# A fused attention-and-convolution block: convolution taps on ScalarE and by adding transfers, and the seven-product pairs regrouped

## The chip, the cores and the metric

The kernel runs on one core of one Trainium2 chip. The metric is the device time of one execution in microseconds (us). TensorE is called PE in the profile, its weight loads PEld, VectorE DVE, ScalarE ACT, GpSimd POOL, and SyncE SP; SP issues most transfers, and POOL issues those that add to what stands in their destination.

## What is computed

One layer over 256 rows (two halves of 128, called h) of width 4096:

```python
xn = rms_norm(h, norm_in_g[i])
proj = xn @ w_in[i]
q, k, v, z_a, a_c, g_c, z_c = jnp.split(proj, ...)
y_a = chunked_attention(q.reshape(shp), k.reshape(shp), v.reshape(shp), rel_table[i])
y_a = rms_norm(y_a, attn_out_g[i]) * jax.nn.silu(z_a)
y_c = conv_module(a_c, g_c, w_dw[i], b_dw[i], conv_ln_g[i], conv_ln_b[i], w_pw[i], b_pw[i])
y_c = rms_norm(y_c, conv_out_g[i]) * jax.nn.silu(z_c)
h = h + jnp.concatenate([y_a, y_c], axis=-1) @ w_out[i]
gate = jax.nn.sigmoid(rms_norm(h, ple_norm_g[i]) @ w_ple_gate[i] + b_ple_gate[i])
h = h + gate * (p[i] @ w_ple[i])
return rms_norm(h, final_g)
```

The module that the change touches is the convolution: `u = a * sigmoid(g)`, then a causal depthwise convolution of 31 taps for each of 2048 channels, a layer norm over the channels, silu, and the product with `w_pw`.

## The kernel before, in words

All large products run on PE as fp32r. A weight tile `wt` of 128 rows and two 512-column blocks comes from memory (SP), ACT casts it to a high part `wh`, DVE subtracts to get the low part `wl`, and PE adds three matmuls of 128x512 (high by high, low by high, high by low) per block. `wpool` holds three `wh` and three `wl`, so the casts run at most a few matmul groups ahead of PE.

`mixed_product` walks over 16 pairs of row blocks in an order written out by hand (`early`, `early_six`, ...). A plain pair takes eight block products, 24 matmuls. A pair with a mark takes seven, 21 matmuls, for which sums of weight blocks (`ua`, `ub`) and combined left operands (`comb`, `comb_x`) are needed. With `*` DVE adds up the weight sums; with `+` an SP transfer fetches the first operand of `ua` and a POOL transfer adds the second to it (`sums_ahead`), and DVE does the rest.

The order of the work is this: the products for the convolution input (`glu_conv(0)` and `(1)`), queries and keys 0, values 0 and 1, attention 0, `glu_conv(2)`, queries and keys 1, attention 1, `glu_conv(3)`, queries and keys 2, queries 3 and values 2, attention 2, `layer_norm_swish`, keys 3 and values 3 (order `norm`), attention 3, and then the product with `w_pw`, whose left operand `uS` is what the layer norm and silu leave. `attention(g)` handles four heads one after the other: scores (two `kT,qT` matmuls per head), DVE adds the bias and finds the maximum, ACT takes the exponential, PE transposes, ACT copies (`pT`), PE multiplies with the values, and ACT scales.

Small work waits in a queue, `later`. After every pair of a product, `fill(n)` takes n entries from its front and writes them into the program; the numbers stand in tables such as `early_fills`, one number per pair. Each `glu_conv` puts 124 entries in it, four blocks of 31 taps (`conv_tap`, each one DVE instruction that multiplies a shifted row by a tap and adds). `layer_norm_swish` puts 71 in it, the last of which are 16 swish entries (a DVE multiplication and an ACT silu each) and 16 split entries (an ACT cast and a DVE subtraction each, which make `uS`). What is still in the queue after attention 3 is written out there, by `fill(len(later))`. A scheduler then sets each engine's order from this program, and each engine works through its own list in that order.

Of the kernel before, what the change touches and what calls it, by code (L numbers as in the profile page):

```python
# [25 lines left out]
def hybrid_block(  # L26
# [23 lines left out]
    nc = tc.nc  # L50
    _, T, D = x.shape
# [5 lines left out]
    TAPS = w_dw.shape[1]  # L57
    PAD = TAPS - 1
# [215 lines left out]
    def sum_rows():  # L274
        return [spool.tile([P, NB], F32, tag="row", name="comb", bufs=3) for _ in range(2)]
# [92 lines left out]
    norm_fills = (7, 8, 8, 8, 6, 4, 2, 3, 2, 3, 2, 2, 0, 6, 5, 5)  # L368
    final = units("1 0* 3 2* 5 4* 6* 7 8* 9 10* 12* 11 13 14 15")
# [2 lines left out]
    def spare_places(tiles):  # L372

        return [[t[:, 0, q, P:] for q in range(2)] for t in tiles]

    places = {}

    def combine_into_places(pair, tiles):

        rows = sum_rows()  # L380
        places[pair] = spare_places(tiles[:4])
        t, i = tiles[pair // 2], pair % 2 * 2
        combine_again(None, None, t, i, rows, at_places=places[pair])()

    def mixed_product(
        w, col, lhs, comb, order, on_helpers, ahead=None, fills=(0,), on_begin=None, apart=NB,
# [252 lines left out]
    def combinations(c, then=lambda ins: None):  # L639
# [8 lines left out]

        return begin, lambda: rest.pop()()

    def first_pairs(add):


# [82 lines left out]
        nc.vector.tensor_reduce(r_x, ssq_x, AX.X, ALU.add)  # L736
        rsqrt(r_x, r_x, D)
        later.extend(combinations(0))
        return n_x + 1, behind

    rows = [(conv_ln_g, KCW), (conv_ln_b, KCW), (b_dw, KCW), (attn_out_g, AW // P),
# [46 lines left out]

    def conv_tap(cv, uT, i, b, k):
        if k == PAD:  # L790
            nc.vector.tensor_scalar(
                cv[:, i, :], uT[:, i, :], dw[:, b, k : k + 1], bdw[:, b : b + 1], ALU.mult, ALU.add
            )
        else:
            nc.vector.scalar_tensor_tensor(  # L795
                cv[:, i, PAD - k :], uT[:, i, : T + k - PAD], dw[:, b, k : k + 1],
                cv[:, i, PAD - k :], ALU.mult, ALU.add,
            )

    def comb_place(where, tag, **kw):  # L800
        return where.tile([P, 2, 2, T], F32R, tag=tag, name="comb_x", **kw), 0

    def more_combinations(pair):

        if pair in (7, 9, 11):
            c = (pair + 1) // 2
            xS[2 * c] = comb_place(act, "act") if c < 6 else comb_place(spool, "hd", bufs=5)
            later.extendleft(reversed(combinations(c)))

    def glu_conv(c):  # L810
        if c == 0:
            sg, gate = scaled_pair(
                w_in0, o_a, o_g - o_a, first, r_x, (1,), begin=first_pairs
            )
        else:
            sg, gate = scaled_pair(
                w_in0, o_a + c * NB, o_g - o_a,
                *((early, r_x, early_fills) if c == 1 else (early_seven, r_x, seven_fills)),
                ahead=more_combinations if c == 2 else None,
            )  # L820
# [303 lines left out]
    r_c = rstd_of(ssq_c, CW, "r_c")  # L1124


    xS = [xS[0][0]]
    for c in range(2, D // NB):
        if c % 2 == 0:
# [306 lines left out]
```

## Time and profile before

| what | value |
|---|---|
| time, median of 3 runs (lowest, highest) | 2023.68 us (2023.65, 2024.45) |
| the profiled execution: time / span | 2023.59 us / 2021.8 us |
| granted TensorE clock, mean | 0.997 |
| PE busy | 2003.7 us, 99% of the span |
| DVE busy | 1920.5 us, 95% |
| ACT busy | 1259.6 us, 62% |
| POOL busy | 75.8 us, 4% |
| transfers | 450.86 MB, 223 GB/s on average |

How to read it: the profiled execution is 0.09 us below the median, and 1.8 us of it lie outside the span. A matmul's record is longer (about 390 ns) than the distance from one matmul to the next, since matmuls overlap. Lines such as L428 are lines of the kernel before; most matmuls come from one helper and share L428.

Windows of the profile in this text go by stages: 97.6 us is the end of `glu_conv(0)`'s product, 889.9 us the end of the product for keys 3 and values 3, and attention 3 lies between 893 and 914 us.

### The profile page before, as it was taken

Reading aid. Unit: us, or ns where it says so; the run is one execution under the profiler, and the core shown is the slowest. Engines: PE = TensorE matmul, PEld = TensorE weight load, DVE = VectorE, ACT = ScalarE, POOL = GpSimd, SP = SyncE. Lnnn points to the kernel's source line nnn. Section 1 sums busy time; section 2 is a strip of 40 time slices with the busy share of each in tenths; the row PEclk is TensorE's granted clock in tenths of the full one; section 3 lists DMA queues with packets and bytes.
Section 4 is the critical chain, followed back from the end, with each engine's and each line's share of the span. In section 5 each row is a group of like instructions: output and inputs, shape, how many; then the busy total and the mean of one; then the engine's idle time right before and its main releaser. Section 6 shows DMA issues by size and latency. Waiting matters only on the chain.

```text
span 2021.8 us, 26364 instructions
## 1 busy us (share of the span) xinstructions
PE 2003.7 (99%) x9043; PEld 1650.4 (82%) x9043; DVE 1920.5 (95%) x2759; ACT 1259.6 (62%) x1634; POOL 75.8 (4%) x83
## 2 busy tenths in 40 slices
PE   9999999999999999999999999999999999999997
PEld 7888888878888888788888888888888888888885
DVE  7999999899999999888999999999999999999997
ACT  7655555665666556776566676776666766566564
POOL 0000000000000000000000000000000000000000
PEclk9999999999999999999999999999999999999998
DMA  8788878678668877556686786876767766767675
GB/s 292 224 233 241 249 221 251 179 220 259 200 198 256 255 201 241 161 178 206 204 238 213 221 244 203 255 232 203 242 209 238 231 197 208 237 214 237 219 238 172
DMA packets 175920, 450.86 MB, mean 223 GB/s; under 512 B 14494, under 2 KB 17710, under 8 KB 175786
## 3 DMA queue, kind: packets, MB, share of 16 engines
q1 hardware_dynamic: 161952, 417.93, 63.6%
q0 software_dynamic: 13184, 30.41, 8.8%
q8 instruction: 71, 1.16, 0.2%
q10 hardware_dynamic: 650, 0.84, 0.1%
q14 instruction: 63, 0.52, 0.1%
HBM read 441.78 MB, written 4.19 MB: 221 GB/s over the span
## 4 chain that ended last, share of the span: by engine, by line
PE 93%; DVE 3%; DMA 2%; issue 2%; ACT 1%; POOLq 0%; POOL 0%; ACTq 0%; DVEq 0%
PE acc L428 70%; PE acc_P L428 18%; PE tmp_ps L170 1%; DVE wl L205 1%; PE acc L245 1%; DMA wt<-in_w_in_dram 1%; DVE cv L795 1%; DMA low<-in_w_in_dram 0%; DVE ul L205 0%; PE tmp_ps L967 0%; PE tmp_ps L951 0%; PE tmp_ps L985 0%; PE tmp_ps L990 0%; DMA wt<-in_w_ple_dram 0%; DMA wt<-in_w_ple_gate_dram 0%
## 5 line engine op out<-in xcount | busy, mean ns | idle before, releaser
L428 PE MATMUL acc<-wh,big_t 128*128 128x512 f32 x4028 | 1240.7, 391 | 0.9 <-DVE z L1146 0.9
L204 ACT CAST wh<-wt 128x1024 fp32r<-128x1024 f32 (+1 forms) x716 | 684.2, 965 | 460.9 <-PE acc L428 336.0
L428 PEld LDWEIGHTS acc<-wh,big_t 128*128 128x128 f32 x4028 | 753.5, 188 | 156.5 <-issue 1.0
L205 DVE TENSOR_TENSOR wl<-wt,wh 128x1024 fp32r<-128x1024 f32 (+1 forms) x716 | 787.9, 1112 | 30.0 <-ACT wh L204 24.8
L428 PE MATMUL acc<-wl,big_t 128*128 128x512 f32 x1958 | 760.3, 392 | 0.2 <-DVE wl L205 0.2
L428 PEld LDWEIGHTS acc<-wl,big_t 128*128 128x128 f32 x1958 | 367.4, 188 | 77.3 <-DVE wl L205 1.5
L204 ACT CAST uh<-ua 128x1024 fp32r<-128x1024 f32 x187 | 196.7, 1052 | 125.3 <-DVE ua L527 71.2
L205 DVE TENSOR_TENSOR ul<-ua,uh 128x1024 fp32r<-128x1024 f32 x187 | 228.0, 1219 | 6.7 <-ACT uh L204 5.1
L795 DVE SCALAR_TENSOR_TENSOR cv<-uT,dw,cv 128x255 f32<-128x255 f32 (+23 forms) x480 | 203.2, 461 | 1.1
L428 PE MATMUL acc_P<-uh,big_t 128*128 128x512 f32 x570 | 175.4, 389 | 0.0
L204 ACT CAST uh<-ub 128x1024 fp32r<-128x1024 f32 x99 | 104.2, 1053 | 51.6 <-DVE ub L540 36.8
L428 PEld LDWEIGHTS acc_P<-uh,big_t 128*128 128x128 f32 x570 | 107.0, 188 | 22.2
L205 DVE TENSOR_TENSOR ul<-ub,uh 128x1024 fp32r<-128x1024 f32 x99 | 120.7, 1219 | 0.5
L428 PE MATMUL acc_P<-ul,big_t 128*128 128x512 f32 x285 | 111.1, 390 | 0.0
L526 DVE TENSOR_TENSOR ua<-wt 128x512 f32<-128x512 f32 x112 | 76.7, 685 | 12.6 <-DMA wt<-in_w_in_dram 6.3
L428 PE MATMUL acc<-uh,big_t 128*128 128x512 f32 x286 | 88.5, 389 | 0.0
L428 PE MATMUL acc_P<-wh,big_t 128*128 128x512 f32 x286 | 88.2, 390 | 0.0
L527 DVE TENSOR_TENSOR ua<-wt 128x512 f32<-128x512 f32 x112 | 76.7, 685 | 4.7 <-DMA wt<-in_w_in_dram 3.5
L428 PE MATMUL acc_P<-uh,comb_t 128*128 128x512 f32 x228 | 70.2, 390 | 0.2 <-ACT uh L204 0.2
L540 DVE TENSOR_TENSOR ub<-ub,wt 128x512 f32<-128x512 f32 x99 | 68.1, 688 | 1.6
L539 DVE TENSOR_TENSOR ub<-ua,wt 128x512 f32<-128x512 f32 x99 | 67.7, 684 | 0.0
L428 PEld LDWEIGHTS acc_P<-ul,big_t 128*128 128x128 f32 x285 | 53.5, 188 | 12.1 <-DVE ul L205 1.0
(254 smaller groups left out, 1634.2 us busy)
## 6 DMA issues: line engine op xcount, KB each, us to landing
wt<-in_w_in_dram SPq DMA_DIRECT2D x416, 512.0 KB, 4.7
wt<-in_w_out_dram SPq DMA_DIRECT2D x128, 512.0 KB, 4.4
wt<-in_w_ple_gate_dram SPq DMA_DIRECT2D x128, 512.0 KB, 4.4
wt<-in_w_pw_dram SPq DMA_DIRECT2D x32, 512.0 KB, 4.5
ua<-in_w_in_dram SPq DMA_DIRECT2D x31, 512.0 KB, 4.3
ua<-in_w_in_dram POOLq DMA_DIRECT2D x31, 512.0 KB, 8.7
wt<-in_w_in_dram SPq DMA_DIRECT2D x31, 256.0 KB, 2.8
low<-in_w_in_dram POOLq DMA_DIRECT2D x12, 512.0 KB, 8.5
```

What stands on the lines that cost most here:

```text
L170: nc.tensor.transpose(pt[:, i * T + h * P : i * T + (h + 1) * P], src[:, h, b] if len(src.shape) == 4 else src[:, h, b * P : (b + 1) * P], ...
L204: nc.scalar.copy(wh[:, :kc, :], wt[:, :kc, :]),
L205: nc.vector.tensor_tensor(wl[:, :kc, :], wt[:, :kc, :], wh[:, :kc, :].bitcast(F32), ALU.subtract),
L245: nc.tensor.matmul(acc, a, b[:, k, :], start=kb == 0 and kind == 0, stop=kb == kblocks - 1 and kind == 2,)
L428: nc.tensor.matmul(banks[name], a, b, start=name not in begun, stop=final and ends[name] == n and kind == 2 and not (left and name in "P2 ...
L526: plus(ua[:, 0], w0[:, 0], w0[:, 1])
L527: plus(ua[:, 1], w0[:, 1], w1[:, 1])
L539: plus(ub[:, 0], ua[:, 0], w1[:, 1])
L540: plus(ub[:, 1], ub[:, 0], w1[:, 0])
L795: nc.vector.scalar_tensor_tensor(cv[:, i, PAD - k :], uT[:, i, : T + k - PAD], dw[:, b, k : k + 1], cv[:, i, PAD - k :], ALU.mult, ALU.add,)
```

## The change

It does four things.

- A block's first tap moves from DVE to ACT. For two of the four blocks of each group, eight taps more become an ACT instruction that writes a scaled, shifted row to a tile `tap` (two buffers, tag `pT`, which attention's `pT` also uses), and a POOL transfer that adds `tap` to `cv`. These rounds stand in `later` after every third DVE tap.
- The operand for pair 8 is combined early, at the end of the first product (`early_places`), so that pair 8 can be a seven from `glu_conv(1)` on; pairs 10 and 12 are combined in `glu_conv(2)` and `glu_conv(3)`.
- The orders change: five sevens instead of four in `glu_conv(1)`, in queries and keys 0 and in values 0 and 1; six instead of seven in `glu_conv(2)`; four as before for queries and keys 1 and 2, the last of them with `*` instead of `+`.
- The fill tables change.

The core of the diff, with what is unchanged or follows from it left out:

```diff
-    early = units("1 3 5 0+ 7 9 2+ 11 13 4+ 15 8 6+ 10 12 14")
-    early_five = units("1 3 5 0+ 7 9 2+ 11 4* 13 6+ 15 8* 10 12 14")
+    early = units("1 3 5 0+ 7 9 2+ 11 13 4+ 15 8 6* 10 12 14")
+    early_five = units("1 3 5 0+ 7 9 2+ 11 8* 13 4+ 15 10 6* 12 14")
...
-    early_fills = (5, 6, 1, 5, 6, 1, 5, 6, 1, 5, 6, 1, 2, 5, 5, 4)
-    six_fills = (6, 6, 1, 5, 1, 5, 1, 5, 1, 5, 1, 5, 1, 6, 7, 7)
-    seven_fills = (6, 6, 1, 5, 1, 5, 1, 5, 1, 5, 1, 2, 5, 2, 5, 7)
+    five_fills = (5, 5, 1, 4, 5, 1, 4, 1, 5, 1, 4, 5, 1, 2, 5, 5)
+    third_fills = (5, 5, 4, 4, 4, 4, 5, 4, 4, 4, 4, 4, 4, 4, 5, 6)
+    early_fills = (5, 6, 1, 5, 5, 1, 5, 5, 1, 5, 5, 1, 2, 5, 4, 4)
+    six_fills = (6, 5, 1, 5, 1, 5, 1, 5, 1, 4, 1, 5, 1, 5, 6, 6)
+    seven_fills = (6, 5, 1, 5, 1, 5, 1, 5, 1, 5, 1, 2, 5, 2, 4, 7)
...
+    def early_places():
...
+            rows = spool.tile([P, 2, NB], F32, tag="stage", name="comb")
+            two = spool.tile([P, 2, 2, P], F32R, name="comb_p", bufs=1)
+            homes = spare_places(xT[:2]) + [[two[:, i, q] for q in range(2)] for i in range(2)]
+            rest.append(combination_in_places(8, xT, (rows[:, 0], rows[:, 1]), homes))
...
         if k == PAD:
-            nc.vector.tensor_scalar(
-                cv[:, i, :], uT[:, i, :], dw[:, b, k : k + 1], bdw[:, b : b + 1], ALU.mult, ALU.add
+            nc.scalar.activation(
+                cv[:, i, :], uT[:, i, :], AF.Identity,
+                scale=dw[:, b, k : k + 1], bias=bdw[:, b : b + 1],
             )
...
+    BY_DMA = 8
...
+    def tap_by_dma(cv, uT, c, i, shift):
+
+        b = 4 * c + i
+        t = spool.tile([P, T], F32, tag="pT", name="tap")
+        nc.scalar.activation(
+            t[:, shift:], uT[:, i, : T - shift], AF.Identity,
+            scale=dw[:, b, PAD - shift : PAD - shift + 1],
+        )
+        nc.gpsimd.dma_start(cv[:, i, shift:], t[:, shift:], accum_op=ALU.add)
...
-    def more_combinations(pair):
-        if pair in (7, 9, 11):
...
+    early_groups = {
+        1: (early_five, r_x, five_fills, None),
+        2: (early_six, r_x, third_fills, more_combinations(9, 10)),
+        3: (early_seven, r_x, seven_fills, more_combinations(11, 12)),
+    }
...
-        for i in range(4):
-            for k in reversed(range(TAPS)):
-                later.append(partial(conv_tap, cv, uT, i, 4 * c + i, k))
+        chain = {i: [partial(conv_tap, cv, uT, i, 4 * c + i, k) for k in reversed(range(TAPS))] for i in range(4)}
+        later.extend(chain[i].pop(0) for i in range(4))
+        rounds = deque((i, shift) for shift in range(1, BY_DMA + 1) for i in (2, 3))
+        for i in (2, 3):
+            del chain[i][:BY_DMA]
+        for n, work in enumerate(chain[0] + chain[1]):
+            later.append(work)
+            if n % 3 == 2 and rounds:
+                later.append(partial(behind_cast, tap_by_dma, cv, uT, c, *rounds.popleft()))
+        later.append(partial(behind_tap, chain[2].pop(0)))
+        later.extend(chain[2])
...
-    heads((o_q, 0), (o_k, 0))
-    heads((o_v, 0), (o_v, 1))
+    heads((o_q, 0), (o_k, 0), order=early_five, fills=five_fills)
+    heads((o_v, 0), (o_v, 1), order=early_five, fills=five_fills)
...
-    moved = comb_place(spool, "hd", bufs=5)
-    nc.scalar.copy(moved[0], xS[10][0])
-    xS[10] = moved
```

What stands in the engines' lists differs at three places of interest. The first is PE's list in attention 3. Before, from the transposes (`ident,s`) of one head to the scores (`kT,qT`) of the next, `acc` being the banks of the product with `w_pw`:

```order
L985 MATMUL tmp_ps<-ident,s 128x128
L428 MATMUL acc_8125<-wh,big_t 128x512 x2
L985 MATMUL tmp_ps<-ident,s 128x128 x2
L428 MATMUL acc_8125<-wl,big_t 128x512
L428 MATMUL acc_8127<-wh,big_t 128x512 x2
L990 MATMUL tmp_ps<-z,pT 128x128
L991 MATMUL tmp_ps<-z,pT 128x128
L992 MATMUL tmp_ps<-z,pT 128x128
L966 MATMUL tmp_ps<-kT,qT 128x128
L967 MATMUL tmp_ps<-kT,qT 128x256
L428 MATMUL acc_8127<-wl,big_t 128x512
```

And PE's list there now, from the layer norm's last small product (`lnsum,mean_w`) and the transposes of the keys (`ident,z`) to the second head's scores:

```order
L960 MATMUL tmp_ps<-lnsum,mean_w 128x128 x2
L1007 MATMUL tmp_ps<-ident,z 128x128 x8
L1022 MATMUL tmp_ps<-kT,qT 128x128
L1023 MATMUL tmp_ps<-kT,qT 128x256
L1041 MATMUL tmp_ps<-ident,s 128x128 x3
L1046 MATMUL tmp_ps<-z,pT 128x128
L1047 MATMUL tmp_ps<-z,pT 128x128
L1048 MATMUL tmp_ps<-z,pT 128x128
L1022 MATMUL tmp_ps<-kT,qT 128x128
```

The matmuls of the product with `w_pw` that stood between the steps of the first three heads are gone from there: before, 59 of them stood ahead of the fourth head's last step, now 14, all in the fourth head.

The second place is ACT's list in attention 3, before, from the copy of the keys through the first head's exponentials (L978) to its last step (L994):

```order
L956 COPY kT<-tmp_ps 128x512 x2
L298 CAST comb_u<-comb 128x2x256
L978 ACT_TABLE_LOAD
L978 ACTIVATE s,den<-s,nm 128x128
L978 ACTIVATE s,den<-s,nm 128x256
L204 CAST wh<-wt 128x1024
L987 COPY pT<-tmp_ps 128x384
L298 CAST comb_u<-comb 128x2x256
L204 CAST wh<-wt 128x1024
L994 ACTIVATE qT<-tmp_ps,den 128x128 x2
```

And now; L966 is the swish entries' silu, which stood ahead of attention 3 before, and L1034 the exponential:

```order
L1012 COPY kT<-tmp_ps 128x512 x2
L966 ACT_TABLE_LOAD
L966 ACTIVATE cv<-cv,prm 128x256
L1034 ACT_TABLE_LOAD
L1034 ACTIVATE s,den<-s,nm 128x128
L1034 ACTIVATE s,den<-s,nm 128x256
L966 ACT_TABLE_LOAD
L966 ACTIVATE cv<-cv,prm 128x256
L1043 COPY pT<-tmp_ps 128x384
L966 ACTIVATE cv<-cv,prm 128x256 x3
L1050 ACTIVATE qT<-tmp_ps,den 128x128 x2
L966 ACTIVATE cv<-cv,prm 128x256 x2
```

The 16 silus now stand between the four heads' exponentials, with eight table loads up to the fourth head's exponential where there was one, and the split casts behind the third head.

The third place is POOL's list from the start, before, with the adding transfers for `ua`:

```order
L134 MEMSET mhalf 128x2
L139 TENSOR_TENSOR r_x<-r_x,mhalf 128x2
L471 DMA ua<-in_w_in_dram 128x2x512 x6
L1017 MEMSET bias 64x4x64
L471 DMA ua<-in_w_in_dram 128x2x512 x11
```

And now, where `tap` are the new adding transfers:

```order
L139 TENSOR_TENSOR r_x<-r_x,mhalf 128x2
L476 DMA ua<-in_w_in_dram 128x2x512 x2
L837 DMA cv<-tap 128x255 x2
L837 DMA cv<-tap 128x254 x2
L476 DMA ua<-in_w_in_dram 128x2x512
L837 DMA cv<-tap 128x253 x2
L837 DMA cv<-tap 128x252 x2
L837 DMA cv<-tap 128x251
L476 DMA ua<-in_w_in_dram 128x2x512
```

Sixteen `tap` transfers per group of channels now share POOL's list with the `ua` transfers.

More of the change, by code (lines that the diff above doesn't have):

```diff
@@ L376, in hybrid_block, with combination_in_places @@
     places = {}
+    def combination_in_places(pair, tiles, rows, homes):
+        places[pair] = homes
+        t, i = tiles[pair // 2], pair % 2 * 2
+        return combine_again(None, None, t, i, rows, at_places=homes)
     def combine_into_places(pair, tiles):
[L380 to L383, printed above, removed]
+        combination_in_places(pair, tiles, sum_rows(), spare_places(tiles[:4]))()
     def mixed_product(
@@ L738, in first_pairs @@
         later.extend(combinations(0))
+        later.extend(early_places())
         return n_x + 1, behind
@@ L790, in conv_tap, with behind_tap, comb_place, more_combinations @@
         if k == PAD:
-            nc.vector.tensor_scalar(
-                cv[:, i, :], uT[:, i, :], dw[:, b, k : k + 1], bdw[:, b : b + 1], ALU.mult, ALU.add
-            )
-        else:
[L795 to L801, printed above, removed]
-    def more_combinations(pair):
-        if pair in (7, 9, 11):
-            c = (pair + 1) // 2
-            xS[2 * c] = comb_place(act, "act") if c < 6 else comb_place(spool, "hd", bufs=5)
-            later.extendleft(reversed(combinations(c)))
+            nc.scalar.activation(
+                cv[:, i, :], uT[:, i, :], AF.Identity,
+                scale=dw[:, b, k : k + 1], bias=bdw[:, b : b + 1],
+            )
+        else:
+            last_tap[:] = [
+                nc.vector.scalar_tensor_tensor(
+                    cv[:, i, PAD - k :], uT[:, i, : T + k - PAD], dw[:, b, k : k + 1],
+                    cv[:, i, PAD - k :], ALU.mult, ALU.add,
+                )
+            ]
+    BY_DMA = 8
+    last_tap = []
+    def behind_tap(work):
+        with tc.issue_after(last_tap[0].ins):
+            work()
+    def tap_by_dma(cv, uT, c, i, shift):
[4 more added lines that the diff above has]
+            scale=dw[:, b, PAD - shift : PAD - shift + 1],
+        )
+        nc.gpsimd.dma_start(cv[:, i, shift:], t[:, shift:], accum_op=ALU.add)
+    def comb_place(where, tag):
+        return where.tile([P, 2, 2, T], F32R, tag=tag, name="comb_x"), 0
+    def more_combinations(at, new):
+        def ahead(pair):
+            if pair == at:
+                xS[new] = comb_place(act, "act")
+                later.extendleft(reversed(combinations(new // 2)))
+        return ahead
+    early_groups = {
[3 more added lines that the diff above has]
+    }
     def glu_conv(c):
@@ L817, in glu_conv @@
                 w_in0, o_a + c * NB, o_g - o_a,
-                *((early, r_x, early_fills) if c == 1 else (early_seven, r_x, seven_fills)),
-                ahead=more_combinations if c == 2 else None,
+                *early_groups[c][:3], ahead=early_groups[c][3],
             )
@@ L838, in glu_conv @@
         cv = act.tile([P, 4, T], F32, tag="act", name="cv")
-        for i in range(4):
-            for k in reversed(range(TAPS)):
-                later.append(partial(conv_tap, cv, uT, i, 4 * c + i, k))
+        chain = {i: [partial(conv_tap, cv, uT, i, 4 * c + i, k) for k in reversed(range(TAPS))] for i in range(4)}
[9 more added lines that the diff above has]
+        later.extend(chain[2])
+        later.append(partial(behind_tap, chain[3].pop(0)))
+        later.extend(chain[3])
         conv.append(cv)
@@ L1124, in hybrid_block @@
     r_c = rstd_of(ssq_c, CW, "r_c")
+    places.pop(8)
     xS = [xS[0][0]]
```

3 lines of the change are left out of this document (added).

## The prediction

> **What bounds the kernel now.** I read the page's busy times first, then the stages' windows, then PE's waits, then the chain of waits around attention 3, the stage that the order of instructions says is rearranged most.
>
> ```profile
> span 2021.8 us, 26364 instructions
> PE 2003.7 (99%) x9043; PEld 1650.4 (82%) x9043; DVE 1920.5 (95%) x2759; ACT 1259.6 (62%) x1634; POOL 75.8 (4%) x83
> ...
> PE 93%; DVE 3%; DMA 2%; issue 2%; ACT 1%; POOLq 0%; POOL 0%; ACTq 0%; DVEq 0%
> ```
>
> PE is busy all but 18.1 us, and 93% of the chain that ended last is PE. DVE at 95% looks like a second bound. What DVE costs PE is read from the nine stages between the end of the first product (97.6 us) and the end of the product for keys 3 (889.9 us), which hold all the convolution taps; the columns are the window, its length, then each engine's busy time:
>
> ```profile
> 183.40:268.90 85.50, 85.50 (x383) 70.80 (x382) 85.50 (x141) 44.28 (x50) 5.17 (x5) 1.00 0.82 240
> ...
> 794.70:889.90 95.20, 94.82 (x443) 77.21 (x442) 84.36 (x141) 71.58 (x120) 1.64 (x1) 1.00 0.56 179
> sum 792.30, PE 790.40 PEld 650.13 DVE 764.49 ACT 461.93 POOL 39.40; mean PE 87.82 PEld 72.24 DVE 84.94 ACT 51.33 POOL 4.38
> ```
>
> In the second row shown first, queries and keys 0, PE and DVE are both busy for 85.5 of 85.5 us; over all nine PE is idle for 792.3 - 790.4 = 1.9 us. Its named waits there are as small:
>
> ```profile
> PE acc_P L428 <- ACT uh L204: 1.6, 3, 0.9
> PE acc_P L428 <- DVE ul L205: 0.2, 1, 0.2
> PE acc L428 <- DVE wl L205: 0.2, 1, 0.2
> ```
>
> So DVE keeps up, just. Relief for DVE can return about 2 us there and no more; only fewer matmuls shorten these stages. Now attention 3, by the chain in order of time (start, length, what):
>
> ```profile
> 893.33 0.49 PE tmp_ps L966 x2
> ...
> 900.10 0.22 PE tmp_ps L966 x2
> ...
> 904.71 0.22 PE tmp_ps L966 x2
> ...
> 909.32 0.22 PE tmp_ps L966 x2
> ...
> 913.14 0.35 PE tmp_ps L990 x2
> 913.49 0.22 PE tmp_ps L991 x2
> 913.72 0.22 PE tmp_ps L992 x2
> 913.94 8.43 PE acc L428 x37
> ```
>
> ```profile
> 893.30:913.90 20.60, 20.57 (x110) 16.52 (x111) 14.11 (x34) 15.14 (x35) 0.00 (x0) 1.00 0.41 134
> ```
>
> Heads start at 893.3, 900.1, 904.7 and 909.3, and PE is through with the fourth at 913.9. The window over all four says that PE is busy for 20.57 of 20.60 us: matmuls of the next product (acc) fill each head's waits. The chain's last row gives the distance of matmuls: 8.43 / 37 = 0.228 us.
>
> **The change, part by part.**
>
> *Sevens.* Marked pairs of the ten products before attention 3 go from 47 to 49 (five instead of four in three products, six instead of seven in one). Each saves three matmuls: 6 x 0.228 = 1.4 us gained. All of it counts, as PE is full there.
>
> *Taps off DVE, sums onto it.*
>
> ```profile
> L795 DVE SCALAR_TENSOR_TENSOR cv<-uT,dw,cv 128x255 f32<-128x255 f32 (+23 forms) x480 | 203.2, 461 | 1.1
> L526 DVE TENSOR_TENSOR ua<-wt 128x512 f32<-128x512 f32 x112 | 76.7, 685 | 12.6 <-DMA wt<-in_w_in_dram 6.3 <-DMA wt<-in_w_ple_gate_dram 4.5 <-DMA wt<-in_w_out_dram 1.6
> L205 DVE TENSOR_TENSOR ul<-ua,uh 128x1024 fp32r<-128x1024 f32 x187 | 228.0, 1219 | 6.7 <-ACT uh L204 5.1 <-PE acc L428 1.2
> L156 ACT ACTIVATE big_t<-tmp_ps,prm 128x256 fp32r<-128x256 f32 x64 | 27.7, 470 | 4.1 <-DVE big_t L157 2.5 <-PE tmp_ps L170 1.6
> hc<-z POOLq DMA_DIRECT2D x12, 256.0 KB, 6.1
> ```
>
> 80 taps at about 0.46 us leave DVE (37 us); 18 more additions for weight sums (12.3 us) and four more low parts (4.9 us) come, so it is relieved by some 20 us in 792. PE gets back about half of its 1.9 us: 1 us gained, between 0 and 1.9.
>
> *Taps on ACT and POOL.* 80 ACT instructions, nearest row 0.47 us, are 38 us, beside 330 us of ACT idle in those stages. The 64 adding transfers are half as large as the 256 KB ones that land after 6.1 us; with two `tap` buffers the tap after next waits in ACT's list for a landing, with weight casts queued behind it. A fill hands out about one round per pair (some 5 us), so the tap after next comes about 10 us later than the first and the landing is in time. Five fewer `ua` transfers pay for part of the traffic. I take 0. From the other side: if one round in each of the four groups is late by a whole landing and PE sees a third of it, that costs 4 x 6.1 / 3, some 8 us.
>
> *The queue runs over.* This decides. The queue receives 4 x 124 tap entries, 71 of the layer norm, and two for each later combination. Before: 573 entries, and the fill tables take 5 x 64 + 58 + 58 + 63 + 71 = 570, so 3 are left at attention 3. Now: 571 entries, and the tables take 3 x 54 + 70 + 60 + 56 + 60 + 58 + 71 = 537. 34 are left: all 16 swishes and 16 splits. They make `uS`, which the product with `w_pw` reads, so its matmuls can no longer fill the heads' waits, and PE's list has none ahead of the fourth head. ACT's list has the silus between the exponentials instead, with a table load at each switch. Durations of these, from ACT's order of time before:
>
> ```profile
> 893.18 0.59 ACT L956 COPY kT<-tmp_ps 128x512 f32<-128x512 f32 x1
> ...
> 894.41 1.28 ACT L978 ACT_TABLE_LOAD   x1
> 895.71 0.40 ACT L978 ACTIVATE s<-s,nm 128x128 f32<-128x128 f32 x1
> ...
> 896.51 0.18 ACT L978 ACTIVATION_READ_ACCUMULATOR s<-s,nm 128x1 f32 x1
> ```
>
> ```profile
> 844.81 1.58 ACT L910 ACTIVATE cv<-cv,prm 128x256 f32<-128x256 f32 x3
> ```
>
> ```profile
> 882.28 1.63 ACT L920 CAST big_t<-cv 128x256 fp32r<-128x256 f32 x5
> ```
>
> ```profile
> 914.13 0.62 ACT L994 ACTIVATE qT<-tmp_ps,den 128x128 f32<-128x128 f32 x2
> ```
>
> ```profile
> L987 ACT COPY pT<-tmp_ps 128x384 f32<-128x384 f32 x16 | 7.7, 478 | 9.7 <-PE tmp_ps L985 9.7
> ```
>
> ACT has the copy of the keys behind it at 893.8. Then, by its new list: load 1.28, one silu 0.6, load 1.28, so the first exponential starts 3.2 us later. From there to the second: exponentials 0.98 (895.71 to 896.69), load 1.28, silu 0.5, copy 0.48, three silus 1.58, the pair of L994 0.62, two silus 1.1, load 1.28: 7.8, less four overlaps of 0.1 (five casts take 1.63): about 7.5 us instead of the 4.6 us from head to head before. The same to the third, 7.2 to the fourth (four splits, 1.3, stand for three silus), then 0.9 of exponentials, three splits 0.9 and the copy, 2.3. Sum 3.2 + 7.5 + 7.5 + 7.2 + 2.3 = 27.7, so 921.5; with the last head's products (0.8, the rows at 913.14) and 0.1 to start them PE is through at 922.4 instead of 913.9: 8.5 us lost. Moreover 59 filling matmuls were done by then and now 14: 45 x 0.228 = 10.3 us to do afterwards. Behind the fourth head's copy ACT has six splits (2.0), two squares (nearest row the copy of 512 columns, 0.59, and a read of 0.18 each), two casts of 512 columns (1.2) and the pair of L994 before the next weight cast (1.2, twice 0.59), 6.5 us, and DVE's low part (1.2) behind it; PE has 0.9 and 22 matmuls, 5.9 us. Between 0 and 1.8 us lost; 1.5, since most of the matmuls there need the cast first.
>
> Table loads at a switch have a page: the Trainium skill (ScalarE: Activation LUTs, What ACT_TABLE_LOAD costs) gives 1.28 us and 1.38 us of drain for a switch of tables. The trace agrees on the load and shows no drain: the exponential starts 0.02 us after it. By the page's 2.66 us, seven more loads would cost another 9.7 us, 2051.1 in all; an estimate that I don't use.
>
> *Sum:* -1.4 - 1.0 + 8.5 + 10.3 + 1.5 = +17.9 on the profiled execution's 2023.59 (0.09 below the median): **2041.5 us**.
>
> **The rivals.**
>
> *A, the forecast:* 2041.5. For it speak the lists, which each engine keeps to. Chance 0.58.
>
> *B, the heads keep their pace of 4.6 us.* Then ACT's silus and loads hide and only the missing filling matmuls cost: 2023.59 + 10.3 - 2.4 = 2031.5. Against it, ACT was idle for 20.6 - 15.1 = 5.5 us there, too little for 16 silus (8 us) and seven more loads (9 us). Chance 0.07.
>
> *C, not slower.* PE would have to get back, in the nine tap stages, what attention 3 loses, by DVE waits that vanish: the chain's 3% of DVE are 60 us on paper. It decides from 17.9 us on, which gives 2023.6. Against it, PE's idle time there is 1.9 us, and the whole span's 18.1. Chance 0.04.
>
> *D, PE's clock falls in attention 3.* For some 20 us PE has only small matmuls, with a gap of some 3.5 us before each head's transposes (ACT's 1.58 + 0.62 + 1.1 + 1.28 + 0.4, less 1.5 of PE's own work). The span's first matmuls of 512 columns, after idleness, are long:
>
> ```profile
> L125 PE MATMUL tmp_ps<-idle 128*128 128x512 bf16 x10 | 4.8, 628 | 1.2 <-DVE ssq_f L1241 1.2
> ```
>
> 628 against some 390 ns. With 0.24 us more for each of the first 15 matmuls afterwards (3.6 us) and 0.5 per head: 2041.5 + 5 = 2046.5. The Trainium skill (TensorE: Matmul & The Clock Gate, Part 1) has a rule to this effect: half the clock after about 3.4 us of idleness, until as long a busy stretch; by it D holds if a gap covers a whole window of its monitor. No run here shows that at the page's figures. Chance 0.22.
>
> *E, the taps' transfers are late*, ACT's casts wait behind them, PE behind those: up to 2041.5 + 8 = 2049.5. POOL's list alternates `tap` with `ua` transfers that wait for SP. Chance 0.09.
>
> **How the numbers follow.** The measurement tells a change of about 0.2%, 4 us, from none. A, B, D and E all lie above that; C's 0.04 is split, 0.02 no change and 0.02 faster, and 0.01 of B goes to no change. Slower 0.95. The low end of the range, 2033, lies between B and A and allows 8 us for steps of ACT that overlap better; the high end, 2052, takes in D and E one at a time. What is left out is B, C and the two together, under 0.2.
>
> **What would show it.** In the profile after: the nine tap stages' lengths within 2 us of before (sevens, E); four heads about 7.5 us apart, PE busy for under a third between the first and the fourth, its transposes waiting for ACT's `s` and its value products for `pT`; 16 table loads instead of 10; a distance of 0.23 us at the first matmuls after the fourth head (against D). I am wrong if the first `w_pw` matmuls stand between the first heads, if the heads are 4.6 us apart, or if the stages before attention 3 shrink by more than 5 us.

## The result: 2.5% slower, and where the time went

The changed kernel takes 2073.69 us (median of four runs, 2071.72 to 2074.24) against 2023.78 for the kernel before beside it: ratio 1.0245, interval 1.0228 to 1.0261. It is 50 us slower; 17.9 were forecast. The profiled execution took 2071.72 us. Its page, the span, the busy times and the chain's engines (the chain reaches back only to 726 us of the span, so its shares don't compare with the 93% of PE before):

```profile
span 2069.9 us, 26521 instructions
...
PE 2019.7 (98%) x9037; PEld 1654.6 (80%) x9037; DVE 1915.3 (93%) x2704; ACT 1296.2 (63%) x1726; POOL 124.7 (6%) x142
...
PE 56%; DVE 4%; ACT 2%; issue 1%; DMA 1%; POOLq 0%; POOL 0%; ACTq 0%; DVEq 0%
```

Six matmuls are gone (9043 to 9037), and PE is idle for 50.2 us instead of 18.1. The same windows as before, from the end of the first product to the end of the ninth stage, show where (queries and keys 0, queries and keys 2, the sum):

```profile
187.20:277.40 90.20, 84.98 (x371) 68.19 (x370) 78.90 (x111) 46.92 (x55) 8.31 (x9) 1.00 0.80 231
...
639.90:734.20 94.30, 89.42 (x385) 72.79 (x384) 84.81 (x135) 51.18 (x64) 11.95 (x13) 0.96 0.84 231
...
sum 817.40, PE 798.67 PEld 650.22 DVE 743.82 ACT 478.04 POOL 88.58; mean PE 88.74 PEld 72.25 DVE 82.65 ACT 53.12 POOL 9.84
```

DVE was relieved by 20.7 us, as computed, yet the nine stages grew from 792.3 to 817.4. PE idles there for 18.7 us instead of 1.9, and in the second row its clock is at 0.96. What is left, from the end of the ninth stage (914.7) to the end of the span, takes 1155.2 us instead of 1131.9. So the loss in this profile is 25.1 us in the tap stages and 23.3 behind them. The waits in the stages, after (total, times, longest):

```profile
DVE wl L205 <- ACT wh L204: 39.7, 28, 7.3
...
ACT tap L833 <- DMA cv<-tap: 30.0, 12, 7.4
...
PE acc L433 <- ACT wh L204: 5.8, 2, 4.8
...
DVE cv L815 <- DMA cv<-tap: 4.5, 4, 3.0
```

The first was 4.8 us before, in the same columns:

```profile
DVE wl L205 <- ACT wh L204: 4.8, 10, 1.3
```

Those on the taps' transfers (`cv<-tap`) are new. The longest of them, in order of time on POOL, ACT and PE:

```profile
713.01 1.23 POOL L476 DMA_DIRECT2D ua<-in_w_in_dram  x1 [9.56 <-DVE z L589]
713.75 1.43 POOL L837 DMA_DIRECT2D cv<-tap  x1
722.42 0.86 POOL L837 DMA_DIRECT2D cv<-tap  x1 [7.23 <-issue]
```

```profile
709.05 0.91 ACT L833 ACTIVATE tap<-uT,dw 128x254 f32<-128x254 f32 x2
...
723.60 0.51 ACT L833 ACTIVATE tap<-uT,dw 128x253 f32<-128x253 f32 x1 [7.44 <-DMA cv<-tap]
...
725.23 1.97 ACT L204 CAST wh<-wt 128x1024 fp32r<-128x1024 f32 x2
```

```profile
721.09 0.39 PE L433 MATMUL acc<-wl,big_t 128*128 128x512 f32 x1
726.31 1.22 PE L433 MATMUL acc<-wh,big_t 128*128 128x512 f32 x2 [4.84 <-ACT wh L204]
```

ACT wrote two taps, at 709.05 and 709.47. POOL's list had a `ua` transfer ahead of theirs, which waited until 713.01. The first tap's transfer, right behind it, landed 9.8 us after its issue, at 723.5; the second's went out at 722.42 only, 0.3 us after the `ua` transfer had landed. ACT's next tap needs the first tile back and waits 7.4 us, the weight copies behind it wait too, and PE stands still. This pattern comes four times in the nine stages, each time where a tap's transfer is issued right behind a `ua` transfer of 512 KB: it lands after 8.2 to 10.4 us (the median of all 64 is 5.0), and POOL's next transfer goes out 0.3 us after the `ua` transfer's landing. Why POOL holds that one back is not shown (the profile says "issue"). The eight tiles of these transfers came back 9.4 to 15.1 us after ACT had written them, the other 56 within 7.6 us. Behind the stall PE runs at half clock, as the windows around it show (PEclk is the third number from the end):

```profile
715.00:725.00 10.00, 6.47 (x29) 5.04 (x27) 4.03 (x8) 2.56 (x5) 1.59 (x3) 1.00 0.88 205
725.00:731.80 6.80, 5.45 (x12) 3.90 (x13) 5.37 (x10) 3.55 (x5) 1.20 (x2) 0.50 0.60 122
```

Attention 3 by the chain, after: the loads of the exponentials' table, the value products of the first head, the last small matmuls, the wait behind them; and the window over the four heads:

```profile
920.70 1.28 ACT L1034
...
925.31 0.80 PE tmp_ps L1046 x2
926.11 0.43 PE tmp_ps L1047 x2
926.53 0.44 PE tmp_ps L1048 x2
...
928.61 1.28 ACT L1034
...
937.02 1.28 ACT L1034
...
950.19 0.24 PE tmp_ps L1048 x2
...
955.17 0.95 ACT wh L204
```

```profile
918.30:950.30 32.00, 18.06 (x67) 12.52 (x68) 16.27 (x52) 29.45 (x61) 0.00 (x0) 0.68 0.11 34
```

The loads stand 7.9 and 8.4 us apart. The value products take 0.80, 0.43 and 0.44 us instead of 0.35, 0.22 and 0.22, at a mean clock of 0.68. ACT is busy for 29.45 of 32.00 us: it is the bound here.

### The profile page after: what moved, and what is told of

It is laid out like the page before. It is cut to its first block, busy times and chain, and to the rows that moved or that the text cites. A ratio compares the mean times of both kernels' runs of the same rounds, so it can differ in the third digit from the quotient of the medians.

```text
span 2069.9 us, 26521 instructions
## 1 busy us (share of the span) xinstructions
PE 2019.7 (98%) x9037; PEld 1654.6 (80%) x9037; DVE 1915.3 (93%) x2704; ACT 1296.2 (63%) x1726; POOL 124.7 (6%) x142
## 4 chain that ended last, share of the span: by engine, by line
PE 56%; DVE 4%; ACT 2%; issue 1%; DMA 1%; POOLq 0%; POOL 0%; ACTq 0%; DVEq 0%
PE acc L433 41%; PE acc_P L433 13%; DVE wl L205 1%; PE acc L245 1%; PE tmp_ps L170 1%; DVE ul L205 0%; DMA wt<-in_w_in_dram 0%; DVE cv L815 0%; DMA low<-in_w_out_dram 0%; ACT wh L204 0%; ACT L966 0%; DVE z L614 0%; DMA wt<-in_w_ple_dram 0%; DMA wt<-in_w_ple_gate_dram 0%; ACT L1034 0%
## 5 line engine op out<-in xcount | busy, mean ns | idle before, releaser
L205 DVE TENSOR_TENSOR ul<-ua,uh 128x1024 fp32r<-128x1024 f32 x191 | 232.9, 1219 | 8.8 <-ACT uh L204 8.3
L815 DVE SCALAR_TENSOR_TENSOR cv<-uT,dw,cv 128x243 f32<-128x243 f32 (+28 forms) x416 | 182.4, 462 | 8.5 <-DMA cv<-tap 4.5
L433 PE MATMUL acc_P<-uh,big_t 128*128 128x512 f32 x594 | 182.7, 389 | 0.0
L433 PEld LDWEIGHTS acc_P<-uh,big_t 128*128 128x128 f32 x594 | 111.4, 188 | 23.3 <-ACT uh L204 0.2
L433 PE MATMUL acc_P<-ul,big_t 128*128 128x512 f32 x297 | 115.7, 391 | 0.2 <-DVE ul L205 0.2
L531 DVE TENSOR_TENSOR ua<-wt 128x512 f32<-128x512 f32 x119 | 81.6, 686 | 13.6 <-DMA wt<-in_w_in_dram 7.6
L532 DVE TENSOR_TENSOR ua<-wt 128x512 f32<-128x512 f32 x119 | 81.5, 685 | 6.1 <-DMA wt<-in_w_in_dram 5.6
L837 POOL DMA_DIRECT2D cv<-tap x64 | 58.1, 909 | 314.5 <-ACT tap L833 281.5
```

The costliest lines, as they stand in the source:

```text
L205: nc.vector.tensor_tensor(wl[:, :kc, :], wt[:, :kc, :], wh[:, :kc, :].bitcast(F32), ALU.subtract),
L433: nc.tensor.matmul(banks[name], a, b, start=name not in begun, stop=final and ends[name] == n and kind == 2 and not (left and name in "P2 ...
L531: plus(ua[:, 0], w0[:, 0], w0[:, 1])
L532: plus(ua[:, 1], w0[:, 1], w1[:, 1])
L815: nc.vector.scalar_tensor_tensor(cv[:, i, PAD - k :], uT[:, i, : T + k - PAD], dw[:, b, k : k + 1], cv[:, i, PAD - k :], ALU.mult, ALU.add,)
L837: nc.gpsimd.dma_start(cv[:, i, shift:], t[:, shift:], accum_op=ALU.add)
```

## Experiments

"Stages" is the length of the nine tap stages and "behind" what follows them, in each kernel's profiled execution. The last columns are what ACT waited for tap tiles and DVE for the taps' transfers in the stages.

| kernel | us, median | ratio to before, interval | stages | behind | ACT | DVE |
|---|---|---|---|---|---|---|
| before | 2023.8 | | 792.3 | 1131.9 | | |
| changed | 2073.7 | 1.0228-1.0261 | 817.4 | 1155.2 | 30.0 | 4.5 |
| drained | 2045.6 | 1.0097-1.0127 | 820.1 | 1130.9 | 41.1 | 6.5 |
| drained late | 2061.3 | 1.0169-1.0206 | 815.6 | 1144.0 | 26.9 | 4.3 |
| busy heads | 2073.2 | 1.0224-1.0255 | 818.9 | 1153.4 | 30.1 | 3.5 |
| no transfers | 2050.5 | 1.0117-1.0147 | 798.1 | 1155.6 | | |
| drained, no transfers | 2030.0 | 1.0019-1.0041 | 799.0 | 1132.0 | | |
| drained, DVE adds | 2027.6 | 1.0010-1.0028 | 797.1 | 1132.5 | 0 | 0 |
| drained, no transfers, four sevens | 2028.2 | 1.0012-1.0031 | 794.8 | 1133.0 | | |
| before, first taps on ACT | 2024.0 | 0.9988-1.0007 | 791.7 | 1132.5 | | |
| four tiles | 2061.7 | 1.0170-1.0200 | 807.9 | 1153.2 | 2.8 | 7.5 |
| drained, four tiles | 2040.9 | 1.0069-1.0099 | 810.2 | 1131.3 | 0 | 8.7 |
| drained, transfers only | 2052.8 | 1.0110-1.0160 | 826.0 | 1131.8 | | 0 |
| four tiles, rounds earlier | 2055.5 | 1.0141-1.0171 | 822.4 | 1132.5 | 0 | 19.3 |
| four tiles, half the rounds | 2028.3 | 1.0009-1.0028 | 797.3 | 1132.4 | 0 | 0 |
| four tiles, transfers last | 2030.8 | 1.0022-1.0045 | 797.2 | 1132.0 | 0 | 6.8 |
| four tiles, transfers last, last group halved | 2022.4 | 0.9986-1.0004 | 792.2 | 1131.6 | 0 | 0 |

The last four are drained, too.

**The queue.** Drained (the tables hand out 31 entries more in all, so 3 are left):

```diff
-    five_fills = (5, 5, 1, 4, 5, 1, 4, 1, 5, 1, 4, 5, 1, 2, 5, 5)
+    five_fills = (5, 6, 1, 5, 5, 1, 5, 1, 5, 1, 5, 5, 1, 2, 5, 5)
```

and likewise 4 more entries in `third_fills`, and the tables of before for the others.

> The fill tables are raised by 20 entries in all, so that 3 entries of the queue are left when attention 3 begins, as in the kernel before, and not 34. Theory Q (the left-over entries make attention 3 long): the time from the end of the ninth tap stage's product to the end of the span falls from 1155.2 us to within 4 us of the 1131.9 us of before, heads follow one another in under 6 us instead of 7.9 to 8.4, and the clock is not halved there; the tap stages keep their sum of about 817 us; about 2050 us in all. Rival (attention 3 is long for another reason, the regrouped orders or the clock alone): the time behind the ninth stage stays within 5 us of 1155, about 2070 us in all.

1130.9 us behind the stages, and the heads' window is that of before to 0.1 us:

```profile
921.00:941.60 20.60, 20.55 (x111) 16.44 (x111) 14.18 (x34) 15.15 (x36) 0.00 (x0) 1.00 0.42 134
```

So the left-over entries make attention 3 long, all of it; the stages keep their loss. Next the same entries, at another place:

```diff
+    fill(len(later) - 3)
     attention(3)
```

> The changed kernel with the 31 entries taken at once, just ahead of attention 3, and 3 left as before. The exponentials then follow one another without silus and table loads between them, and the first product behind them has its operands, so filling matmuls stand between the heads again. If the loss is the mixing of silus and exponentials in ScalarE's list and the missing fillers: heads 4.6 to 5 us apart, 10 or 11 table loads in all, but a first head later by 16 silus and 16 splits (about 13 us, less what the end of the product before hides): 8 to 13 us lost behind the ninth stage instead of 23.4, about 2058 to 2063 us in all. If it is the work itself being late, whatever its order: 2070 or more.

12.1 us are lost behind the stages instead of 23.3. The chain shows what is paid: all silus in one piece ahead of the first head, with one load; then fillers stand between the heads again.

```profile
918.84 7.97 ACT cv L966 x16
926.81 0.92 ACT big_t L976 x3
927.73 0.04 issue
927.77 4.87 PE acc L433 x14
```

About half of the loss, then, goes when silus and exponentials are not mixed in ACT's list and fillers stand between the heads, two things that this run does not tell apart. The other half stays when the work comes late in one piece; PE's clock is at half for 10.2 us of it (920.45 to 930.7), the 14 matmuls of the last row included.

> The changed kernel, 34 entries left, with 16 more small matmuls (128x128, into unused columns of the scores' bank, never read) in each of the four heads of attention 3, 8 behind the scores and 8 behind the transposes: PE is kept busy for some 3.5 us of each head's waits. Theory D (the halved clock is part of the 23.4 us that attention 3 loses): the clock stays whole there, the value products take 0.35 and 0.22 us again, the heads follow in 7.5 instead of 7.9 to 8.4 us, and the time behind the ninth stage falls from 1155.2 by 2 to 4 us. Rival (the clock is only seen there, ScalarE's chain sets the pace): the clock stays whole and the time stays within 1 us of 1155.

```diff
+    def busy(g, sp, a, b):
+        for _ in range(8 if g == 3 else 0):
+            nc.tensor.matmul(sp[:, P + T :], a, b, start=True, stop=True)
...
+            busy(g, sp, qT[:, hd, :P], kT[:, hd, :P])
```

Inconclusive. The value products of the second head are at 0.22 us again, but each 8 of the added matmuls (L1020, counted double) take 1.78 us and stand in the chain themselves:

```profile
938.83 0.22 PE tmp_ps L1054 x2
939.06 0.22 PE tmp_ps L1055 x2
...
939.94 1.78 PE tmp_ps L1020 x16
```

1153.4 us lies between two kernels without them that leave the same entries (1153.2 and 1155.6). The clock was at half for 3.4 us there (930.2 to 933.6) instead of 20.5 (923.0 to 936.6 and 940.1 to 946.9), and PE was through with the fourth head 36.2 us after the ninth stage's end, against 35.7 in the changed kernel: a whole clock together with these matmuls gained the heads nothing.

**Transfers or sevens.** All taps but the first of each block back on DVE, alone and with the drained queue:

```diff
-    BY_DMA = 8
+    BY_DMA = 0
```

> The 64 taps that went over ScalarE and an adding transfer are VectorE's again; the first tap of each block stays ScalarE's, sevens and tables stay those of the changed kernel. VectorE gets about 64 x 0.46 = 29 us of work in the nine stages, 744 to 773 of 817. Theory W: no wait for tap tiles is left, the stages' sum falls by 10 to 20 us to about 800, 2055 to 2062 us in all. Theory S: the stages get no shorter, or longer by up to 15 us, as VectorE has still less room around the sevens: 2072 to 2088 us.

> Both edits: the queue is drained before attention 3 (3 entries left) and all taps but each block's first are VectorE's. Q with W: both losses go, the stages' sum is about 795 to 800 and what follows 1132 to 1136, 2028 to 2038 us. Q with S: the stages' sum stays 815 to 835 and only attention 3 recovers, 2050 to 2068 us. W without Q: 2055 to 2062 us.

DVE has 767 us in the stages instead of 744, and they are 19 us shorter. The transfers' taps cost about 19 of the 25 us, with the extra sevens in place. Is it ACT's scaling or the transfer?

```diff
-        nc.gpsimd.dma_start(cv[:, i, shift:], t[:, shift:], accum_op=ALU.add)
+        nc.vector.tensor_tensor(cv[:, i, shift:], t[:, shift:], cv[:, i, shift:], ALU.add)
```

> Drained queue. ScalarE scales the 64 taps as in the changed kernel, into the same two tiles, but VectorE adds them to the sums (64 additions in place of 64 adding transfers), so ScalarE's list and its work stay, and no adding transfer of a tap is left. Theory T (the loss in the stages is the wait for the transfers' landing): the stages fall from 820 to within 4 us of the 799 of the kernel with all taps on VectorE, about 2030 us in all. Theory A (it is ScalarE's 64 x 0.50 us ahead of weight copies): the stages stay at 808 to 820, 2038 to 2046 us.

```profile
sum 797.07, PE 791.75 PEld 650.16 DVE 772.22 ACT 494.57 POOL 33.32; mean PE 87.97 PEld 72.24 DVE 85.80 ACT 54.95 POOL 3.70
```

ACT does all of the scaling, 495 us busy, and the stages are as short as without it: theory A falls. The loss is in the transfers and the waits for them.

Then the sevens, with the order and the fills of before (`early` there) in the three groups that got a fifth marked pair, and `BY_DMA = 0` and the drained queue as above:

```diff
-        1: (early_five, r_x, five_fills, None),
+        1: (early_four, r_x, early_four_fills, None),
...
-    heads((o_q, 0), (o_k, 0), order=early_five, fills=five_fills)
+    heads((o_q, 0), (o_k, 0), order=early_four, fills=early_four_fills)
...
```

> Drained queue, all taps but each block's first on VectorE, and the three groups with five marked pairs back to the four marked pairs of before (9 more matmuls of 0.228 us, 2.1 us; pair 8 is combined but not used). Theory S (the fifth pair costs more in VectorE's time around it than its matmuls save; it is the 6.3 us that the kernel with both edits still loses to before): the stages fall from 799 to 793 to 796 us, 2023 to 2027 us in all. If the fifth pair pays: 2032 us.

The stages get 4.2 us shorter in the profile, but the medians differ by 1.7 us and their intervals overlap: the fifth marked pairs gain nothing here with DVE this full, and what they lose isn't measured. The first taps alone, in the kernel before:

```diff
-            nc.vector.tensor_scalar(
-                cv[:, i, :], uT[:, i, :], dw[:, b, k : k + 1], bdw[:, b : b + 1], ALU.mult, ALU.add
-            )
+            nc.scalar.activation(
+                cv[:, i, :], uT[:, i, :], AF.Identity,
+                scale=dw[:, b, k : k + 1], bias=bdw[:, b : b + 1],
+            )
```

> The kernel before with one part of the change alone: the first tap of each of the 16 blocks on ScalarE instead of VectorE (7 us less for VectorE, 10 us more for ScalarE). If the taps on ScalarE are harmless by themselves, and PE gets back at most half of its 1.9 us: 2022 to 2024 us. If ScalarE's list is too full for them: over 2026 us.

No change, as both the row (DVE 764 to 759 us) and PE's idle 1.9 us led one to expect.

**What in the transfers.** Twice the tiles, with and without the drained queue:

```diff
-        t = spool.tile([P, T], F32, tag="pT", name="tap")
+        t = spool.tile([P, T], F32, tag="pT" if i == 2 else "s", name="tap")
```

> The scaled taps for the adding transfers get four tiles instead of two (those of the third block stay in one pair, those of the fourth take the pair that only attention uses); nothing else changes. Theory W (ScalarE waits in its own list for a tap's tile, the weights' copies stand behind it, TensorE runs dry and then at half clock): ScalarE's wait for tap tiles falls from 30.0 us to under 6, PE's stall of 5.0 us at 721 and the half clock after it go, and the nine stages' 817 us shrink by 8 to 20; about 2055 to 2062 us. Theory S (the extra sevens need too much of VectorE at once, whatever the taps do): the stages stay within 4 us of 817, about 2072 us. Attention 3 is as in the changed kernel under both.

> The drained queue and the four tap tiles together. If the queue and the tap tiles are separate causes, their gains add: 2045.6 - (2073.7 - 2061.7) = about 2034 us, nine stages about 808 us, 1131 us behind them. If the draining by itself made the stages different (they were 820 us with two tiles), 2040 or more.

ACT's wait is gone (all but 2.8 us in the first), the stall at 721 too, and the stages are shorter by 9.5 and 9.9 us. The medians fall by 12.0 and 4.8, and the 2034 us expected were missed: the drained kernel's profiled execution, 2050.4 us, was the longest of its four (from 2045.2), so the tiles are worth between 5 and 12 us. Some 11 to 13 remain against the kernels without transfers. DVE's wait, POOL and DVE in the drained kernel with four tiles:

```profile
DVE cv L815 <- DMA cv<-tap: 8.7, 3, 4.5
```

```profile
187.49 0.87 POOL L837 DMA_DIRECT2D cv<-tap  x1 [0.92 <-ACT z L868]
189.71 0.86 POOL L837 DMA_DIRECT2D cv<-tap  x1 [1.35 <-DMA cv<-tap]
194.08 0.86 POOL L837 DMA_DIRECT2D cv<-tap  x1 [3.52 <-DMA cv<-tap]
```

```profile
196.19 0.99 DVE L815 SCALAR_TENSOR_TENSOR cv<-uT,dw,cv 128x247 f32<-128x247 f32 x2 [5.29 <-issue]
```

A transfer waits in POOL's list until the one before it into the same block has landed. The two shown last are the last into the two blocks. The one of 189.71 lands at 196.0, 6.3 us after its issue, and until then DVE stands for 5.3 us (put down to issue, so not in the table) before its own taps of that block (247 columns: the ninth shift, the first that stays with DVE). With the 8.7 us, DVE's waits for a block's last transfer come to 14.0 us in the stages. That gave theory L. First the transfers without ACT's scaling (this kernel leaves the multiplication out, so what it computes is not the layer):

```diff
-        t = spool.tile(...)
-        nc.scalar.activation(t[:, shift:], uT[:, i, : T - shift], ...)
-        nc.gpsimd.dma_start(cv[:, i, shift:], t[:, shift:], accum_op=ALU.add)
+        nc.gpsimd.dma_start(cv[:, i, shift:], uT[:, i, : T - shift], accum_op=ALU.add)
```

> Drained queue. The 64 adding transfers read the gated input itself and ScalarE's scaling is left out (so these taps go in unscaled): no tap tile, no wait of ScalarE, but the same transfers on POOL's queue at the same places. Theory T (ScalarE's wait for a landing): nobody on ScalarE waits, the stages are 795 to 801 us, 2026 to 2032 us in all. Rival P (the transfers themselves cost: they delay the weights' adding transfers in POOL's list, or VectorE waits for them): the stages stay above 806, 2037 us or more.

Theory T alone falls: worse, 826 us, by another way. Nothing paces the transfers on POOL now, they wait there for each other, and the weight sums behind them come late; ACT's copies of these wait up to 9.5 us:

```profile
POOL cv L832 <- DMA cv<-uT: 85.5, 41, 5.5
...
ACT uh L204 <- DMA ua<-in_w_in_dram: 33.2, 4, 9.5
```

Then the rounds after every second tap:

```diff
-            if n % 3 == 2 and rounds:
+            if n % 2 == 1 and rounds:
```

> Drained queue and four tap tiles, and the 16 adding transfers of a group are handed out after every second of VectorE's taps instead of every third, so the last one is issued some 16 taps earlier (some 9 us or more). Theory L (what four tiles leave of the loss is VectorE's wait for the last transfers of a group: each waits in POOL's list until the one before into the same block has landed, and VectorE's own taps of that block stand behind them; 5.3 and 4.5 us in two groups): VectorE's waits there fall under 2 us in all, the nine stages from 810 to 799 to 804 us, 2029 to 2035 us in all. Rival C (the transfers cost by their traffic or by POOL's list, wherever they stand): the stages stay at 808 to 814 us, 2038 to 2044 us.

This edit did the opposite of what I meant. The transfers still went out at the pace of POOL's and ACT's lists, about one pair in 9 us. In three of the four groups the last one into the first block did land 10 to 29 us sooner than in the kernel with four tiles, but DVE came to the block sooner, too, by 6 to 32 us, for a reason that is not shown. Its waits grew to 19.3 us:

```profile
DVE cv L815 <- DMA cv<-tap: 19.3, 4, 6.5
```

The mechanism was there four times, but the run told L and C apart in neither way. Two others do:

```diff
-    BY_DMA = 8
+    BY_DMA = 4
```

> Drained queue and four tap tiles, with 4 adding transfers into each of the two blocks of a group instead of 8 (VectorE gets the other 32 taps, 15 us in nine stages). The transfers keep a pace of about one pair in 9 us, so a group's last one is issued some 35 us earlier against VectorE's list. Theory L (what is left of the loss with four tiles is VectorE's wait for a group's last transfers, on which its own taps of the block stand): VectorE waits for them under 2 us in all instead of 9, the nine stages fall from 810 to 798 to 802 us, 2028 to 2033 us in all. Rival C (each transfer costs the same wherever it stands): half of the 11 to 13 us stays, stages 804 to 806, 2034 to 2037 us.

```diff
+        later.extend(chain[2] + chain[3])
         for n, work in enumerate(chain[0] + chain[1]):
...
-        later.append(partial(behind_tap, chain[2].pop(0)))
-        later.extend(chain[2])
```

(and likewise for `chain[3]`):

> Drained queue, four tap tiles and all 64 transfers, but VectorE's taps of the two blocks with transfers come first in each group and those of the two others behind them, with the transfers among these: nothing on VectorE waits for a transfer before the layer norm. Theory L: VectorE's waits for transfers are gone, the nine stages fall from 810 to 798 to 803 us, 2028 to 2034 us in all. Rival C (traffic, POOL's list or ScalarE's part): the stages stay at 808 to 814 us, 2038 to 2044 us.

Both give 797 us. With all 64 transfers kept and only the order of DVE's taps and the transfers changed, the stages are as short as without any: a price for each transfer wherever it stands (C) falls. Transfers last has one wait left, and it shows what the term is worth: DVE's layer norm asks for the last group's sum.

```profile
DVE lnsum L925 <- DMA cv<-tap: 6.8, 1, 6.8
```

PE stood 5.8 us there and ran at half clock for 6.8 behind it. Without it:

```diff
+        by_dma = BY_DMA if c < 3 else BY_DMA // 2
```

> As with the transfers last, but the fourth group has 4 transfers into each of its two blocks instead of 8, so that its last one lands before the layer norm's first sum asks for it (it waited 6.8 us for it, PE stood 5.8 us and then ran at half clock for 6.8). Theory L to the end: that wait is gone, the last two stages fall from 188.0 to about 180 us, and since the first seven stages were 3.4 us shorter than before's, the nine come to 788 to 791 us against 792.3, about 2020 to 2022 us in all: faster than the kernel before by 0.1 to 0.2%. Rival (the first seven stages' gain is this profile's luck, or the fourth group's end is bound elsewhere): 2024 us or more.

```profile
sum 792.17, PE 790.48 PEld 648.41 DVE 750.69 ACT 490.74 POOL 82.79; mean PE 87.83 PEld 72.05 DVE 83.41 ACT 54.53 POOL 9.20
```

The stages are those of before (792.3), with 56 transfers, the fifth sevens and 14 us less of DVE. 2022.4 us is no change against before (0.9986 to 1.0004), and the gain of 0.1 to 0.2% that I expected did not come: PE is busy for 790.5 of 792.2 us, so freed DVE time buys nothing. No version here beats the kernel before.

## Why the prediction was right and wrong

- *Sevens, -1.4:* the matmul count fell by six. The time never showed: PE lost more by waiting, and where it waited no more than before (the last kernel of the table, idle for 1.7 us) the stages are 0.1 us shorter and the median 1.3 us lower, which is within the noise.
- *DVE's relief, -1.0:* the 20 us were right (20.7). The return was bounded rightly, at PE's idle 1.9 us: first taps alone, and the last kernel of the table with 14 us of relief, are no change.
- *Taps on ACT and POOL, 0, up to 8: this step failed.* The stages grew by 25.1 us in the profile, three times the upper bound. 19 us of it go with the transfers, and all of it goes when 56 transfers stay but nobody stands behind them (792.2, the last kernel). Three assumptions were wrong. "The tap after next comes about 10 us later than the first and the landing is in time": the distance held on average (a median of 12.9 us), but 19 of 56 were shorter than 10 us, and eight of the 64 tiles took 9.4 to 15.1 us to come back, around the four places where a tap's transfer follows a `ua` transfer in POOL's list. Three waits for such tiles make 15.1 of ACT's 30.0 us, those where taps came close together the rest (all of them are worth 5 to 12 us of time, by four tiles). A transfer's landing was counted once, but eight into one block wait for each other, and DVE's own taps of that block wait for the eighth; the bound had no term for DVE at all (half the rounds and transfers last took away 10 to 13 us). And a stall of PE was priced at its length, while half clock can follow it. Rival E named ACT's wait and POOL's list, at 8 us and a chance of 0.09; size and chance were far too small.
- *The queue, +20.3:* the mechanism was right and the size nearly: 23.3 measured, 24.3 given back by draining. Counting 34 entries in the fill tables was enough. By its terms: PE is through with the fourth head 35.7 us after the ninth stage's end (950.43) instead of 24.0, 11.7 us lost where 8.5 were computed; the rest, 11.6, stands against 10.3 + 1.5. Of the signs named, the 16 table loads instead of 10 came as said; the heads' loads stood 7.9 and 8.4 us apart, not 7.5, and PE was busy for about half of the time between the first head and the fourth (11.7 of 24.2 us), not a third, much of it at half clock.
- *Rival D, the clock:* it came, in attention 3 and behind the stalls in the stages. In attention 3 it would account for most of the 3.2 us that were missing: the value products take 1.67 instead of 0.79 us in each of three heads, on the chain, 2.6 us. That is read from the chain and not shown by an experiment: the run meant to test it did not settle it. The Trainium skill's rule (TensorE: Matmul & The Clock Gate, Part 1) names the effect; what this case adds is below.
- *Table loads:* the Trainium skill's drain behind a table load (ScalarE: Activation LUTs, What ACT_TABLE_LOAD costs) was rightly left out: the load at 920.70 takes 1.28 us and the exponential starts at 922.00, 0.02 us later.
- *Not slower (C), heads at their old pace (B):* neither came.

## What to carry to other kernels

Moving work from a full engine to an idle one by a transfer pays only where nobody waits for the landing: put the work that reads the result last, give each transfer in flight a tile, and look at what stands in the same engine's list ahead of each transfer and behind each wait. Where transfers add into one place, count their landings one after the other, and let the last consumer be far. And count the entries of a work queue against what the tables take out: a few left over can cost more than the change was meant to gain.

## What the runs showed of the hardware

- The adding transfers of about 125 KB take POOL 0.87 us to issue and land after a median of 5.0 us, 2.6 to 10.4 us (64 in the changed kernel); the four longest are those right behind a 512 KB one in POOL's list, 8.2 to 10.4 us. Their waits are paid on the issuing engine: POOL waited for the transfer before 41 times in the kernel without scaling (85.5 us). The Trainium skill (DMA: Bandwidth & Descriptors, Anatomy of one DMA) says the same, that a transfer's semaphore wait is held by the sequencer that issues it; the trace agrees.
- Gaps of PE shorter than the window of 3.4 us that the Trainium skill gives (TensorE: Matmul & The Clock Gate, Part 1) halved the clock in some places as well. In the kernel where DVE adds, half clock followed a gap of 1.9 us, though PE was full on both sides, and lasted 3.4 us (the rows below). Gaps of 2.2 and 1.8 us in the changed kernel (at 191.3 and 239.6) were followed by no half clock; what tells the two apart is not shown:

```profile
627.31 0.70 PE L433 MATMUL acc<-wh,big_t 128*128 128x512 f32 x2 [1.89 <-DVE z L614]
```

```profile
620.00:627.90 7.90, 6.01 (x27) 4.67 (x26) 7.90 (x14) 4.39 (x6) 0.00 (x0) 1.00 1.04 300
627.90:631.30 3.40, 3.40 (x10) 2.63 (x9) 3.40 (x6) 2.21 (x3) 1.22 (x1) 0.50 0.53 198
631.30:640.00 8.70, 8.70 (x44) 7.23 (x43) 7.57 (x13) 6.57 (x10) 0.31 (x1) 1.00 0.97 256
```
